# Decoder layer on one core: ten groups of seven products in the second half of each down product, four blocks with five such groups in the first gate/up, earlier folds in the second

## The chip, the core and the metric

The kernel runs on one core of a Trainium2 chip. Its time is the device time of one launch in microseconds (us). Engines: the PE (TensorE) multiplies, DVE (VectorE) adds and subtracts, ACT (ScalarE) casts, copies and evaluates functions, POOL (GpSimd) issues the accumulating DMAs here, and SP (SyncE) issues the loads.

## The reference

One layer for 256 tokens of width 2048, all in float32: a half feed-forward, a mix of retention and windowed attention, a second half feed-forward, and a gated embedding, each followed by a layer norm. The change touches the two feed-forwards:

```python
D_MODEL, SEQ, D_FF = 2048, 256, 5632

def swiglu(x, w_gu, w_down):
    g, u = jnp.split(x @ w_gu, 2, axis=-1)
    return (jax.nn.silu(g) * u) @ w_down

h = layer_norm(alpha * h + 0.5 * swiglu(h, w_ffn1_gu, w_ffn1_down), ...)
...   # retention, attention, mix
h = layer_norm(alpha * h + 0.5 * swiglu(h, w_ffn2_gu, w_ffn2_down), ...)
```

w_gu is 2048 x 11264, w_down 5632 x 2048.

## The kernel before

**Precision.** A float32 product is made of three matmuls on rounded halves: x = hi + lo, and hi·lo, hi·hi and lo·hi are added up in PSUM (`Sum.add`, L510 to L512). The activations' halves stay in memory; each weight chunk (128 x 1024, 512 KB) is loaded once, rounded by ACT (`hf`, L162) and its rest formed by DVE (`lf`, L164). The names of tiles begin with r (raw, as loaded), h and l; `f1_gu_3_0_4` in such a name is the first feed-forward's gate/up, block 3, gate (0) or up (1) columns, pair 4 of the inner dimension.

**Kinds of units.** A stage's inner dimension goes by pairs of 128 rows. For each pair and for a 2 x 2 block of outputs (two halves of the tokens, two groups of 512 columns) there is one unit, and a string of letters says which kind:

- P: two chunks, each split by ACT and DVE; 24 matmuls.
- F: the same 24 matmuls, but the second chunk's rest is made by a fold: ACT multiplies the raw chunk by -1 (`Folding`, L181), POOL issues a DMA that adds the rounded one to it (L182), and ACT makes hi later (`Folded`, L198). It costs DVE one split rather than two.
- S: a group of seven products in place of eight (Strassen's scheme in Winograd's form): 21 matmuls. The weights' sums are made by DVE and ACT: five DVE operations on 512 columns (L279, L280, L285, L289, L294), three on 1024 (L287 `lf`, L296 `luf`, L298 `lvf`), and four casts on ACT (L277, L278, L284 `huf`, L293 `hvf`). The activations' sums ("forms") are made once for each pair. Four extra sums in PSUM (tiles named with s) collect the shared products, and after the last S of a block ACT and DVE combine them (L634, L635, L637 to L639).

**Stages.** A feed-forward has gate/up blocks 0 to 10 of 512 gate and 512 up columns with eight pairs each, then the down product in two halves of 1024 columns with 22 pairs each: the first is written by FIRST_DOWN, the second by SECOND_DOWN, whose last two (f1) or three (f2) pairs are held for the layer norm's part. Gate/up blocks go by `gu_units`: f1's blocks 1 to 10 are "FFSSFSSP"; f2's block 9 is "FSSFSSSP", with a fifth S, for the pair SEVEN_MORE = 4. Each block's gate and up are multiplied and transposed by DMA, and come back as the activations of the down product.

**What sets the order.** All units of the kernel stand in one list, `plan`. `fill` goes ahead of the PE: it issues loads and makes splits in the order of the plan, as long as slots in memory are left (`room`; `slots_for_weights` sets their number by stage, `others` in the down product) and as long as the prepared time is below `ahead`. An S holds seven slots until the PE is done with it, a P's chunk two. `fold_at` puts the begun fold some units ahead of its place: it goes back until the units between take FOLD_AHEAD of time, and in a stretch with S groups on to the next S before that. With FOLD_AHEAD of 0 the multiplication is right ahead of the use. `weave` lets DVE steps of a finished block slip between the steps of a split. All engines run their instructions in the order written, and DVE's, ACT's and SP's lists are set by this plan.

At the start of a second down product DVE first combines the sums of the first (L635 to L639), adds the residual (L1206), adds the other sums (L1241), and takes the statistics (L916).

Of the kernel before, what the change touches and what calls it, by code (L numbers as in the profile page):

```python
# [9 lines left out]
F32R = mybir.dt.float32r  # L10
# [6 lines left out]
P = 128  # L17
S = 256
# [9 lines left out]
KF = FF // P  # L28
# [10 lines left out]
SLOTS = 46  # L39


FOLD_AHEAD = {"f1_gu": 34, "f1_down": 12, "f2_gu": 0, "f2_down": 12}

SEVEN = (0, 1, 2, 3)

# [4 lines left out]

ASIDE_TO = 8

FIVE = {"f1": (), "f2": (9,)}

DELAY = {"f1": 2, "f2": 1}

SEVEN_DOWN = (6, 7, 8, 9)

FIRST_DOWN = "PPPPPFFSFSFSPSFSPSFSPS"
SECOND_DOWN = "PPPSPSPSFSPSFSSPSPPPPP"  # L60
LEAD = 4

BIG = 3.0e38
# [7 lines left out]
def layer(ctx: ExitStack, tc: tile.TileContext, io):  # L71
# [4 lines left out]
    big = ctx.enter_context(tc.tile_pool(name="big", bufs=1))  # L76
# [11 lines left out]
    def slot(shape, dt, name):  # L88
        return slots.tile(shape, dt, tag="slot", name=name)
# [111 lines left out]
    def fold_at(ahead, key):  # L201

        begun = Folding(key)
        at, time = len(plan), 0
        while at > 0 and time < ahead:
            at -= 1
            time += plan[at].time
        if ahead and any(isinstance(u, Seven) for u in plan[at - 12 : at + 1]):
            while not isinstance(plan[at], Seven):
                at -= 1  # L210
        plan.insert(at, begun)
        plan.append(Folded(begun))
# [222 lines left out]
    def slots_for_weights(n, ahead=45, far=90):  # L435
        room.update(slots=n, ahead=ahead, far=far)

    def quiet(on):
        room["quiet"] = on
# [92 lines left out]
    def block_units(units, keys):  # L532

        for kind, p in units:
            if kind == "P":
                plan.extend(Single(keys(n, p)) for n in range(2))
            elif kind == "F":
                plan.append(Single(keys(0, p)))
                fold_at(FOLD_AHEAD[keys(1, p)[0]], keys(1, p))
            else:  # L540
# [39 lines left out]
    def forms_sums(full):  # L580


        n = full.shape[1] // 2
        a11, a21 = (full[:, 0::2, t * P : (t + 1) * P] for t in range(2))
        a12, a22 = (full[:, 1::2, t * P : (t + 1) * P] for t in range(2))
        raw = slot([P, 4 * n, P], F32, "sums")
        f5, f6, f7, f3 = (raw[:, n * j : n * j + n, :] for j in range(4))
        dve.tensor_tensor(f5, a21, a22, ALU.subtract)
        dve.tensor_tensor(f7, a11, a21, ALU.subtract)
        dve.tensor_tensor(f6, f5, a11, ALU.subtract)  # L590
        dve.tensor_tensor(f3, a12, f6, ALU.add)
        return raw

    def forms_split(raw, hi, lo):

        split(hi, lo, raw)
        n = raw.shape[1] // 4
        return lambda e: [(hi[:, n * j + e, :], lo[:, n * j + e, :]) for j in range(4)]

    def seven_forms(full, hi, lo, between=None):  # L600

        raw = forms_sums(full)
        if between is not None:
            between()
        return forms_split(raw, hi, lo)
# [13 lines left out]
    def units_of(order, sevens, ahead=()):  # L619

        sevens, ahead = list(sevens), list(ahead)
        plain = [p for p in range(KD // 2) if p not in sevens + ahead]
        of = {"S": sevens, "D": ahead, "P": plain, "F": plain}
        return [(kind, of[kind].pop(0)) for kind in order]
# [293 lines left out]
    def load_columns(src, col, name):  # L918
        v = slot([P, 2, 512], F32, f"{name}{col}")
        sync.dma_start(v, src[col])  # L920
        return v
# [4 lines left out]
    def load_for_norm(i):  # L926

        vectors.append(ln_vectors(i))
        if i < 2:
            p_raws.append(slot([P, 2, S], F32, "praw"))  # L930
            sync.dma_start(p_raws[0], io["pT"])

    def make_for_norm():
        if p_raws:
            raw, pt = p_raws.pop(), slot([P, 2, 512], F32R, "pt")
            split(pt[:, :, :S], pt[:, :, S:], raw)
            p_parts.append(pt)
# [35 lines left out]
    ht = big.tile([P, KD, 512], F32R, tag="ht", name="xt")  # L973
# [50 lines left out]
    def gu_units(name, j):  # L1024
        if j == 0:
            return [("P", p) for p in range(KD // 2)]
        if name == "f2" and j in AHEAD:
# [3 lines left out]
            return units_of(*((f"P{plain}SDSDSP", SEVEN[:3]) if j % 2 else (f"P{plain}SSDSSP", SEVEN)), AHEAD[j])  # L1031
        if j in FIVE[name]:
            return units_of("FSSFSSSP", SEVEN + (SEVEN_MORE,))
# [6 lines left out]
    def down_units(n_held):  # L1040


        sevens = [2 * g + e for g in SEVEN_DOWN for e in range(2)]
        plain = [p for p in range(KF // 2) if p not in sevens]
        first, second = [], []
        for out, order in ((first, FIRST_DOWN), (second, SECOND_DOWN)):
            n = order.count("S")
            of = {"S": sevens[:n], "P": sorted(plain + sevens[n:], key=lambda p: (p in sevens, p))}
            of["F"] = of["P"]
            out += [(kind, of[kind].pop(0)) for kind in order]  # L1050
            assert not of["S"] and not of["P"]
        return first, second[:-n_held], [p for _, p in second[-n_held:]]
# [4 lines left out]
    def plan_ffn(name):  # L1057
        for j in range(KF // 4):
            block_units(gu_units(name, j), gu_keys(name, j))
        first, second, held = down_units(HELD_PAIRS[name == "f2"])  # L1060
        block_units(first, down_keys(name, 0))
        block_units(second, down_keys(name, 1))
        plan.extend(Single(down_keys(name, 1)(n, p)) for n in range(2) for p in held)

    def ffn(name, i, ht, norm, keep, residual, keepers, away):
# [3 lines left out]
        raws = {}  # L1069
        made = {}  # L1070
# [45 lines left out]
        acts = {}  # L1116

        def convert_high(g):
            hi, lo = (slot([P, 4, S], F32R, f"{name}a{w}{g}") for w in "hl")
            act.copy(hi, raws[g])  # L1120
            acts[g] = hi, lo
            return lambda: dve.tensor_tensor(lo, raws[g], hi, ALU.subtract)
# [4 lines left out]
        for j in range(KF // 4):  # L1127
# [22 lines left out]
            def before(u, j=j, offset=KD // 2 - len(units)):  # L1150
# [7 lines left out]
                if j == 0 and u == 7:  # L1158
                    for g in sorted({p // 2 for p in SEVEN}):
                        hi, lo = (slot([P, 8, P], F32R, f"{name}f{w}{g}") for w in "hl")  # L1160
                        made[g] = seven_forms(keep[g], hi, lo)
                    if FIVE["f1"] and name == "f1":
                        both = slot([P, 2, 4, P], F32R, "f1fm")
# [23 lines left out]
        def others(n, ahead=45):  # L1187

            slots_for_weights(SLOTS - 4 - n - (2 if lazy else 0), ahead, max(90, ahead + 12))

        lhs = lambda k: tuple(a[:, k % 4, :] for a in acts[k // 4])
        y = {}
        space = big.tile([P, 2 * len(SEVEN_DOWN), 8, P], F32R, tag="ht", name=name + "forms")
        made = {}
        first, second, held = down_units(HELD_PAIRS[name == "f2"])
        n_of = {}
        for b, units in enumerate((first, second + [("P", p) for p in held])):
# [17 lines left out]

        def before_unit(u):
            new = [g for g in when if when[g] == u]
            others(2 * KF // 4 - (KF // 4 - len(acts) - len(new)) + (2 if u >= 10 else 0))
            lows = [convert_high(g) for g in new]

            def convert_low():
                for f in lows:
                    f()

            if u % 2 == 0 and 2 <= u < 2 + 2 * len(SEVEN_DOWN):
                at = u // 2 - 1
                made[SEVEN_DOWN[at]] = seven_forms(
                    raws[SEVEN_DOWN[at]], space[:, 2 * at], space[:, 2 * at + 1], convert_low
                )
            else:  # L1230
                convert_low()
            if u in (11, 12):
                y[u - 11] = load_columns(residual, u - 11, name + "y")

        pn = [banks(f"{name}d{n}") for n in range(2)]
        sums = [[Sum(pn[n][t], n_of[0][t, n]) for n in range(2)] for t in range(2)]
        block(f"{name}d0", first, down_keys(name, 0), lhs, forms, sums, fold(0), before_unit)
        weave_all()
        for n in range(2):
# [6 lines left out]
        last_ahead = 136  # L1246
        last = {}
# [1 line left out]
            last[p // 2] = at  # L1249

        def before_unit(u):
            others(2 * sum(at >= u for at in last.values()) + (4 if u < 12 else 9), 45 if u < len(second) - 5 else last_ahead)
            if u in (11, 12):
                y[u - 9] = load_columns(residual, u - 9, name + "y")
            if u == 13:
                load_for_norm(i)
            if u == len(second) - 1:
                make_for_norm()
                quiet(i < 2)

        pt_ = [banks(f"{name}e{t}") for t in range(2)]
        sums = [[Sum(pt_[t][n], n_of[1][t, n]) for n in range(2)] for t in range(2)]
        block(f"{name}d1", second, down_keys(name, 1), lhs, forms, sums, fold(1), before_unit)
        weave_all()
        slots_for_weights(27, last_ahead, last_ahead + 24)
# [803 lines left out]
```

## Time and profile before

| | |
|---|---|
| median of 3 runs | 2228.23 us (2227.85 to 2229.13) |
| profiled execution | 2227.33 us, its span 2225.5 us |
| granted clock of the PE | 0.999 |
| busy: PE, PE weight load | 2214.5 us (100%), 1836.3 us (83%) |
| busy: DVE, ACT, POOL | 1996.5 us (90%), 1452.4 us (65%), 51.0 us (2%) |
| DMA | 575.49 MB, mean 259 GB/s |

Shares are of the span. A busy time counts an engine's instructions without its waits; the PE's matmuls overlap, so their durations add up to more than its time, and what one more of them costs is read from the distance of their starts. A line such as `L635 ... [3.25 <-PE f13s L512]` in a timeline says that the engine sat idle for 3.25 us before this instruction, and that the last thing it waited for was the matmul of L512 on tile f13s. In the list of waits a row has the waiting instruction, what it waited for, the total in us, how often, and the longest.

### The profile page before, as it was taken

Reading aid. Unit: us, or ns where it says so; the run is one execution under the profiler, and the core shown is the slowest. Engines: PE = TensorE matmul, PEld = TensorE weight load, DVE = VectorE, ACT = ScalarE, POOL = GpSimd, SP = SyncE. Lnnn points to the kernel's source line nnn. Section 1 sums busy time; section 2 is a strip of 40 time slices with the busy share of each in tenths; the row PEclk is TensorE's granted clock in tenths of the full one; section 3 lists DMA queues with packets and bytes.
Section 4 is the critical chain, followed back from the end, with each engine's and each line's share of the span. In section 5 each row is a group of like instructions: output and inputs, shape, how many; then the busy total and the mean of one; then the engine's idle time right before and its main releaser. Section 6 shows DMA issues by size and latency. Waiting matters only on the chain.

```text
span 2225.5 us, 29118 instructions
## 1 busy us (share of the span) xinstructions
PE 2214.5 (100%) x10125; PEld 1836.3 (83%) x10125; DVE 1996.5 (90%) x2654; ACT 1452.4 (65%) x1687; POOL 51.0 (2%) x65
## 2 busy tenths in 40 slices
PE   9999999999999999999999999999999999999998
PEld 8888888888888888888788888888888878888887
DVE  6989989989988889789999888779999999899887
ACT  6877777776565545557866567466767678765553
POOL 0000000000000000000000000000000000000000
PEclk9999999999999999999999999999999999999999
DMA  9998998977686889846976578888899899777871
GB/s 312 279 267 243 248 278 229 257 222 249 219 307 235 302 280 330 273 170 226 294 231 234 172 219 319 307 302 265 293 310 312 289 261 276 213 237 238 290 284 68
DMA packets 303771, 575.49 MB, mean 259 GB/s; under 512 B 98812, under 2 KB 103804, under 8 KB 303624
## 3 DMA queue, kind: packets, MB, share of 16 engines
q1 hardware_dynamic: 293576, 541.70, 73.0%
q0 software_dynamic: 8064, 29.36, 7.0%
q10 hardware_dynamic: 1984, 2.58, 0.3%
q8 instruction: 79, 1.29, 0.2%
q14 instruction: 68, 0.56, 0.1%
HBM read 490.20 MB, written 33.55 MB: 235 GB/s over the span
## 4 chain that ended last, share of the span: by engine, by line
PE 95%; DMA 2%; DVE 1%; issue 1%; ACT 0%; ACTq 0%; SPq 0%; DVEq 0%; POOLq 0%
PE f1g L510 3%; PE f1g L512 3%; PE f1g L511 3%; PE rqk L461 3%; PE f1u L510 2%; PE f1u L511 2%; PE f1u L512 2%; PE f2g L512 2%; PE f2g L510 2%; PE f2g L511 2%; PE f2u L512 2%; PE f2u L510 2%; PE f2u L511 2%; PE aqk L461 2%; PE f2e L512 1%; PE f2e L511 1%
## 5 line engine op out<-in xcount | busy, mean ns | idle before, releaser
L164 DVE TENSOR_TENSOR lf_gu<-rf_gu,hf_gu 128x1024 fp32r<-128x1024 f32 x126 | 150.0, 1227 | 29.7 <-ACT hf_gu L162 28.9
L164 DVE TENSOR_TENSOR lw_in_f<-rw_in_f,hw_in_f 128x1024 fp32r<-128x1024 f32 x132 | 158.3, 1221 | 13.6 <-ACT hw_in_f L162 13.5
L162 ACT CAST hf_gu<-rf_gu 128x1024 fp32r<-128x1024 f32 x126 | 127.7, 1050 | 37.6 <-DMA rf_gu<-in_f_gu 31.3
L162 ACT CAST hw_in_f<-rw_in_f 128x1024 fp32r<-128x1024 f32 x132 | 132.9, 1052 | 6.6 <-DMA rw_in_f<-in_w_in_f 3.8
L164 DVE TENSOR_TENSOR lf_down<-rf_down,hf_down 128x1024 fp32r<-128x1024 f32 x96 | 115.9, 1224 | 19.5 <-ACT hf_down L162 16.7
L293 ACT CAST hvf_gu<-vf_gu 128x1024 fp32r<-128x1024 f32 x80 | 84.5, 1056 | 68.7 <-DVE vf_gu L289 65.1
L284 ACT CAST huf_gu<-uf_gu 128x1024 fp32r<-128x1024 f32 x80 | 84.4, 1055 | 65.1 <-DVE uf_gu L280 62.8
L162 ACT CAST hf_down<-rf_down 128x1024 fp32r<-128x1024 f32 x96 | 98.7, 1050 | 25.4 <-DMA rf_down<-in_f_down 12.0
L287 DVE TENSOR_TENSOR lf_gu<-rf_gu,hf_gu 128x1024 fp32r<-128x1024 f32 x80 | 98.1, 1227 | 0.3
L298 DVE TENSOR_TENSOR lvf_gu<-vf_gu,hvf_gu 128x1024 fp32r<-128x1024 f32 x80 | 98.3, 1229 | 0.0
L296 DVE TENSOR_TENSOR luf_gu<-uf_gu,huf_gu 128x1024 fp32r<-128x1024 f32 x80 | 98.3, 1228 | 0.0
L510 PE MATMUL f1g<-hf_gu,xt 128*128 128x512 f32 x232 | 90.5, 390 | 0.4 <-ACT hf_gu L113 0.4
L512 PE MATMUL f1g<-lf_gu,xt 128*128 128x512 f32 x232 | 90.4, 390 | 0.0
L511 PE MATMUL f1g<-hf_gu,xt 128*128 128x512 f32 x232 | 90.3, 389 | 0.0
L277 ACT CAST hf_gu<-rf_gu 128x1024 fp32r<-128x1024 f32 x80 | 83.8, 1048 | 4.6 <-DMA rf_gu<-in_f_gu 4.6
L510 PE MATMUL f2g<-hf_gu,ht 128*128 128x512 f32 x196 | 76.4, 390 | 0.0
L512 PE MATMUL f2g<-lf_gu,ht 128*128 128x512 f32 x196 | 76.3, 389 | 0.0
L511 PE MATMUL f2g<-hf_gu,ht 128*128 128x512 f32 x196 | 76.2, 389 | 0.0
L510 PE MATMUL f1u<-hf_gu,xt 128*128 128x512 f32 x192 | 74.7, 389 | 0.0
L511 PE MATMUL f1u<-hf_gu,xt 128*128 128x512 f32 x192 | 74.7, 389 | 0.0
L512 PE MATMUL f1u<-lf_gu,xt 128*128 128x512 f32 x192 | 74.7, 389 | 0.0
L182 POOL DMA_DIRECT2D lf_gu<-rf_gu x40 | 34.8, 870 | 1632.5 <-PE f2g L511 991.6
(1546 smaller groups left out, 7205.6 us busy)
## 6 DMA issues: line engine op xcount, KB each, us to landing
rf_gu<-in_f_gu SPq DMA_DIRECT2D x362, 512.0 KB
rf_down<-in_f_down SPq DMA_DIRECT2D x176, 512.0 KB
rw_in_f<-in_w_in_f SPq DMA_DIRECT2D x148, 512.0 KB
lf_gu<-rf_gu POOLq DMA_DIRECT2D x40, 512.0 KB, 8.3
rw_rv<-in_w_rv SPq DMA_DIRECT2D x32, 512.0 KB
rw_ret<-in_w_ret SPq DMA_DIRECT2D x32, 512.0 KB
rw_mix<-in_w_mix SPq DMA_DIRECT2D x32, 512.0 KB
rw_pg<-in_w_pg SPq DMA_DIRECT2D x32, 512.0 KB
```

The lines of the kernel that those rows point to most:

```text
L162: act.copy(c.hi, c.raw)
L164: dve.tensor_tensor(c.lo, c.raw, c.hi, ALU.subtract)
L277: act.copy(a.hi, a.raw)
L284: act.copy(uh, u)
L287: dve.tensor_tensor(a.lo, a.raw, a.hi, ALU.subtract)
L293: act.copy(vh, v)
L296: dve.tensor_tensor(ul, u, uh, ALU.subtract)
L298: dve.tensor_tensor(vl, v, vh, ALU.subtract)
L461: pe.matmul(ps[f], hi[:, kk, f * P : (f + 1) * P], rhs(k), start=k == 0, stop=k == n_k - 1,)
L510: pe.matmul(o, al, bh, start=first, stop=False)
L511: pe.matmul(o, ah, bh, start=False, stop=False)
L512: pe.matmul(o, ah, bl, start=False, stop=self.left == 0)
```

## The change

Four tables of letters and numbers change, with what goes along with them:

```diff
-FOLD_AHEAD = {"f1_gu": 34, "f1_down": 12, "f2_gu": 0, "f2_down": 12}
+FOLD_AHEAD = {"f1_gu": 34, "f1_down": 12, "f2_gu": 12, "f2_down": 12}
...
-FIVE = {"f1": (), "f2": (9,)}
+FIVE = {"f1": (3, 5, 7, 9), "f2": (9,)}
...
-SEVEN_DOWN = (6, 7, 8, 9)
-
-FIRST_DOWN = "PPPPPFFSFSFSPSFSPSFSPS"
-SECOND_DOWN = "PPPSPSPSFSPSFSSPSPPPPP"
+SEVEN_DOWN = (6, 7, 8, 9, 5)
+
+FIRST_DOWN = "PPPPFFFSFSFSFSFSPSFSPS"
+SECOND_DOWN = "PPSPSPSFSFSFSSFSSSPPPP"
...
-            of = {"S": sevens[:n], "P": sorted(plain + sevens[n:], key=lambda p: (p in sevens, p))}
+            of = {"S": sevens[:n], "P": sorted(plain + sevens[n:])}
...
-        space = big.tile([P, 2 * len(SEVEN_DOWN), 8, P], F32R, tag="ht", name=name + "forms")
+        space = big.tile([P, 8, 8, P], F32R, tag="ht", name=name + "forms")
...
-            others(2 * KF // 4 - (KF // 4 - len(acts) - len(new)) + (2 if u >= 10 else 0))
+            others(2 * KF // 4 - (KF // 4 - len(acts) - len(new)) + (4 if u >= 10 else 0))
...
-                made[SEVEN_DOWN[at]] = seven_forms(
-                    raws[SEVEN_DOWN[at]], space[:, 2 * at], space[:, 2 * at + 1], convert_low
-                )
+                if at < 4:
+                    hi, lo = space[:, 2 * at], space[:, 2 * at + 1]
+                else:
+                    hi, lo = (slot([P, 8, P], F32R, f"{name}f{w}{u}") for w in "hl")
+                made[SEVEN_DOWN[at]] = seven_forms(raws[SEVEN_DOWN[at]], hi, lo, convert_low)
...
-            others(2 * sum(at >= u for at in last.values()) + (4 if u < 12 else 9), 45 if u < len(second) - 5 else last_ahead)
+            others(2 * sum(at >= u for at in last.values()) + (6 if u < 12 else 11), 45 if u < len(second) - 5 else last_ahead)
```

In f1's blocks 3, 5, 7 and 9 one F becomes an S ("FFSSFSSP" becomes "FSSFSSSP"); the forms of its pair are made in block 0. In the first down product two P become F, with eight S as before; in the second two P become S and two become F (8 S to 10). The fifth group of forms, for activations 5, takes two slots from the pool that the weights share, made at unit 10, so the weights have two fewer from there. f2's folds in gate/up are begun earlier. In all, the PE's rows go from 9942 to 9918, and DVE's from 2592 to 2651.

DVE at the end of f1's block 3, before: the last S (pair 3), then the splits of pair 7 and the first split of block 4, then the combining of block 3's sums.

```order
L296 TENSOR_TENSOR luf1_gu_3_0_3_1441<-uf1_gu_3_0_3_1431,huf1_gu_3_0_3_1440 128x1024
L298 TENSOR_TENSOR lvf1_gu_3_0_3_1447<-vf1_gu_3_0_3_1432,hvf1_gu_3_0_3_1446 128x1024
L164 TENSOR_TENSOR lf1_gu_3_0_7_1467<-rf1_gu_3_0_7_1365,hf1_gu_3_0_7_1466 128x1024
L164 TENSOR_TENSOR lf1_gu_3_1_7_1492<-rf1_gu_3_1_7_1411,hf1_gu_3_1_7_1491 128x1024
L164 TENSOR_TENSOR lf1_gu_4_0_4_1519<-rf1_gu_4_0_4_1452,hf1_gu_4_0_4_1518 128x1024
L635 TENSOR_TENSOR evw_1531<-eve_1530,f13s1_1339 128x512
```

The same place now:

```order
L298 TENSOR_TENSOR lvf1_gu_3_0_3_1412<-vf1_gu_3_0_3_1397,hvf1_gu_3_0_3_1411 128x1024
L279 TENSOR_TENSOR uf1_gu_3_0_4_1437<-rf1_gu_3_1_4_1335 128x512
L280 TENSOR_TENSOR uf1_gu_3_0_4_1437<-rf1_gu_3_0_4_1333,rf1_gu_3_1_4_1335 128x512
L285 TENSOR_TENSOR vf1_gu_3_0_4_1438<-rf1_gu_3_0_4_1333,uf1_gu_3_0_4_1437 128x512
L287 TENSOR_TENSOR lf1_gu_3_0_4_1441<-rf1_gu_3_0_4_1333,hf1_gu_3_0_4_1440 128x1024
L289 TENSOR_TENSOR vf1_gu_3_0_4_1438<-vf1_gu_3_0_4_1438,rf1_gu_3_0_4_1333 128x512
L294 TENSOR_TENSOR bf1_gu_3_0_4_1439<-rf1_gu_3_1_4_1335,bf1_gu_3_0_4_1439 128x512
L296 TENSOR_TENSOR luf1_gu_3_0_4_1447<-uf1_gu_3_0_4_1437,huf1_gu_3_0_4_1446 128x1024
L298 TENSOR_TENSOR lvf1_gu_3_0_4_1453<-vf1_gu_3_0_4_1438,hvf1_gu_3_0_4_1452 128x1024
L164 TENSOR_TENSOR lf1_gu_3_0_7_1484<-rf1_gu_3_0_7_1382,hf1_gu_3_0_7_1483 128x1024
```

Eight DVE instructions for pair 4 stand between pair 3 and pair 7; the one split of pair 4 at the start of the block is gone.

DVE at the start of f1's second down product, before: the end of the statistics, the two splits of the third P (pair 2), and the first S (pair 12).

```order
L916 BN_STATS f1st_4098<-f1y1_4662 128x6 x2
L164 TENSOR_TENSOR lf1_down_2_2_5102<-rf1_down_2_2_5015,hf1_down_2_2_5101 128x1024
L164 TENSOR_TENSOR lf1_down_3_2_5120<-rf1_down_3_2_5033,hf1_down_3_2_5119 128x1024
L279 TENSOR_TENSOR uf1_down_2_12_5135<-rf1_down_3_12_5066 128x512
L280 TENSOR_TENSOR uf1_down_2_12_5135<-rf1_down_2_12_5064,rf1_down_3_12_5066 128x512
```

The same place now:

```order
L916 BN_STATS f1st_4147<-f1y1_4717 128x6 x2
L279 TENSOR_TENSOR uf1_down_2_12_5152<-rf1_down_3_12_5117 128x512
L280 TENSOR_TENSOR uf1_down_2_12_5152<-rf1_down_2_12_5115,rf1_down_3_12_5117 128x512
L285 TENSOR_TENSOR vf1_down_2_12_5153<-rf1_down_2_12_5115,uf1_down_2_12_5152 128x512
L287 TENSOR_TENSOR lf1_down_2_12_5156<-rf1_down_2_12_5115,hf1_down_2_12_5155 128x1024
```

The first S comes right behind the statistics, two splits sooner on DVE, and on the PE one P sooner.

ACT in f2 between block 8 and block 9, before: the fold of pair 5 of block 9 (L181, then L198) stands right ahead of the combining of block 8's sums (L634).

```order
L162 CAST hf2_gu_8_1_7_16301<-rf2_gu_8_1_7_16249 128x1024
L162 CAST hf2_gu_9_0_5_16330<-rf2_gu_9_0_5_16251 128x1024
L181 ACTIVATE lf2_gu_9_1_5_16334<-rf2_gu_9_1_5_16278 128x1024
L198 CAST hf2_gu_9_1_5_16337<-rf2_gu_9_1_5_16278 128x1024
L634 COPY eve_16343<-f28s0_16155 128x512
```

Now:

```order
L181 ACTIVATE lf2_gu_9_1_5_16307<-rf2_gu_9_1_5_16278 128x1024
L277 CAST hf2_gu_8_0_3_16313<-rf2_gu_8_0_3_16280 128x1024
L278 CAST bf2_gu_8_0_3_16312<-rf2_gu_8_1_3_16282 128x512
L284 CAST huf2_gu_8_0_3_16319<-uf2_gu_8_0_3_16310 128x1024
L293 CAST hvf2_gu_8_0_3_16325<-vf2_gu_8_0_3_16311 128x1024
L162 CAST hf2_gu_8_0_7_16356<-rf2_gu_8_0_7_16284 128x1024
L162 CAST hf2_gu_8_1_7_16381<-rf2_gu_8_1_7_16331 128x1024
L162 CAST hf2_gu_9_0_5_16410<-rf2_gu_9_0_5_16333 128x1024
L198 CAST hf2_gu_9_1_5_16414<-rf2_gu_9_1_5_16278 128x1024
L634 COPY eve_16422<-f28s0_16232 128x512
```

The multiplication, and with it POOL's DMA, stands ahead of block 8's last S (pair 3), seven casts sooner.

## The prediction

> **What bounds the kernel now.** I read the page first, then the waits of the PE, then the stages that the change touches by windows, and there the timelines of DVE, ACT and PE. The page has the shares and the chain:
>
> ```profile
> span 2225.5 us, 29118 instructions
> PE 2214.5 (100%) x10125; PEld 1836.3 (83%) x10125; DVE 1996.5 (90%) x2654; ACT 1452.4 (65%) x1687; POOL 51.0 (2%) x65
> PE 95%; DMA 2%; DVE 1%; issue 1%; ACT 0%; ACTq 0%; SPq 0%; DVEq 0%; POOLq 0%
> ```
>
> The chain runs through the PE for 95% of the span. The waits of the PE hold seven rows; the largest, and the only one on a split of a weight by DVE, are
>
> ```profile
> PE f2u L512 <- DMA lf_gu<-rf_gu: 1.8, 3, 1.1
> PE mr1a L512 <- DVE lw_ret L164: 0.5, 1, 0.5
> ```
>
> so in the stages of the change the PE waits only for three folds of the second layer's gate/up. Windows (length; then busy time and count of PE, PEld, DVE, ACT, POOL; clock, DMA share, GB/s) of an f1 block of four, the one block of five that exists (f2 9), two S groups on DVE inside it, and the two second down products:
>
> ```profile
> 339.70:380.50 40.80, 40.80 (x182) 33.80 (x181) 36.58 (x46) 30.12 (x32) 2.59 (x3) 1.00 0.93 258
> 1808.00:1850.00 42.00, 40.35 (x175) 32.31 (x174) 41.77 (x52) 30.54 (x34) 1.74 (x2) 1.00 0.89 257
> 1831.92:1844.70 12.78, 12.78 (x58) 10.58 (x57) 12.78 (x17) 7.10 (x9) 0.00 (x0) 1.00 0.97 267
> 571.50:686.00 114.50, 114.50 (x507) 94.85 (x506) 104.97 (x127) 63.68 (x69) 1.75 (x2) 1.00 0.77 267
> 2008.00:2124.00 116.00, 116.00 (x517) 96.10 (x517) 107.64 (x132) 64.58 (x71) 1.91 (x3) 1.00 0.75 261
> ```
>
> PE is full in all but the block of five, DVE is close behind it. A group of seven trades PE time for DVE time, and the question is whether DVE has it to give.
>
> **The change part by part.** *Matmuls removed.* Eight pairs go from 24 matmuls (P or F) to 21 (S): four in f1's gate/up and two in each second down product, 24 matmuls in all. The price of one:
>
> ```profile
> L510 PE MATMUL f1g<-hf_gu,xt 128*128 128x512 f32 x232 | 90.5, 390 | 0.4 <-ACT hf_gu L113 0.4
> 572.16 0.39 PE L510 MATMUL f1e<-hf_down,f1al 128*128 128x512 f32 x1
> 583.04 0.39 PE L510 MATMUL f1e<-hf_down,f1al 128*128 128x512 f32 x1
> ```
>
> The two starts in the second product stand 48 matmuls (two P) apart: 10.88 / 48 = 0.2267 us a matmul, though each lasts 0.39 us. So 24 matmuls are 24 x 0.2267 = 5.44 us. By their durations they would be 24 x 0.39 = 9.4 us. The Trainium skill ("Perfetto Trace Analysis", Identifying the Most-Contended Engine) says that matmul busy time is no measure, because matmuls are pipelined; by that rule 5.44 is the sum to take, and these rows agree with it.
>
> *What DVE pays.* The window of two S groups gives 12.78 / 2 = 6.4 us for one. The operations of one length in it:
>
> ```profile
> L279 DVE TENSOR_TENSOR uf_gu<-rf_gu 128x512 f32<-128x512 f32 x5 | 3.5, 691 | 0.0
> L298 DVE TENSOR_TENSOR lvf_gu<-vf_gu,hvf_gu 128x1024 fp32r<-128x1024 f32 x5 | 6.1, 1228 | 0.0
> ```
>
> They overlap their neighbours by some 0.09 us (1843.85 to 1844.99, 1.14, in the rows below). An F costs one such split, 1.14 us, a P two, 2.27. F to S costs DVE 5.27 us, P to S 4.14, and P to F gives 1.14 back.
>
> *Blocks of five in f1.* What DVE has to spare in a block of four stands just ahead of L635, where it waits for the last S sums of the PE; beside it the same place ahead of f2's block of five, and that block's end:
>
> ```profile
> 164.44 0.69 DVE L635 TENSOR_TENSOR evw<-eve,f13s 128x512 f32<-128x512 f32 x1 [3.25 <-PE f13s L512]
> 164.62 0.39 PE L512 MATMUL f13s<-luf_gu,f1fh 128*128 128x512 f32 x1
> 327.63 0.69 DVE L635 TENSOR_TENSOR evw<-eve,f17s 128x512 f32<-128x512 f32 x1 [2.18 <-PE f17s L512]
> 1803.23 0.40 PE L512 MATMUL f28s<-luf_gu,f2fh 128*128 128x512 f32 x1
> 1805.86 0.69 DVE L635 TENSOR_TENSOR evw<-eve,f28s 128x512 f32<-128x512 f32 x1
> 1843.85 1.24 DVE L298 TENSOR_TENSOR lvf_gu<-vf_gu,hvf_gu 128x1024 fp32r<-128x1024 f32 x1
> 1844.99 1.24 DVE L164 TENSOR_TENSOR lf_gu<-rf_gu,hf_gu 128x1024 fp32r<-128x1024 f32 x1
> 1845.21 0.43 PE L512 MATMUL f29s<-lvf_gu,f2f2h 128*128 128x512 f32 x1
> ```
>
> From L635 to the end of the fifth lv DVE works without a gap: 1843.85 + 1.24 - 1805.86 = 39.2 us. The PE starts the last S sum of the block before at 1803.23 and reads that lv 174 matmuls later, 174 x 0.2267 = 39.45 us if nothing holds it. So a block of five costs the PE what L635 starts late after that matmul, less 0.2: here 2.63, and the PE lost 41.98 - 39.45 = 2.5. In f1, where DVE has been waiting, L635 even starts 0.18 ahead of that matmul (164.44 against 164.62): no loss, but only 0.4 us of margin. The extra 5.27 us leave DVE 5.27 - 3.25 + 3 x 0.2267 = 2.7 late at the end of a block of five, and the block of four behind it has 3.25 to give (2.18 at the end of block 7): that is why only every second block can be one. Two of the four start late in before, for a chunk that comes late to ACT:
>
> ```profile
> 241.79 1.05 ACT L162 CAST hf_gu<-rf_gu 128x1024 fp32r<-128x1024 f32 x1 [2.25 <-DMA rf_gu<-in_f_gu]
> 285.25 1.05 ACT L162 CAST hf_gu<-rf_gu 128x1024 fp32r<-128x1024 f32 x1 [2.86 <-PE f16s L511]
> 287.77 0.69 DVE L635 TENSOR_TENSOR evw<-eve,f16s 128x512 f32<-128x512 f32 x1 [0.21 <-ACT eve L634]
> ```
>
> Three blocks of 40.80 after 164.62 the same matmul of block 6 stands at 287.02, so L635 ahead of block 7 is 0.75 late, some 0.55 of stall if block 6 ends that way again. Blocks 3 and 5 have their L635 in time. I take 0.7 us for the four together: 12 x 0.2267 - 0.7 = **2.0** us gained. Ends: nothing lost (2.7), or 2.5 lost in each as in f2 9 (2.7 - 10 = -7.3). I stay near the first, since L635 waits for the PE in f1 and for ACT in f2 8. The forms for the fifth pair (four 128x128 operations, one of 512, one cast on ACT, in block 0) stand where DVE has no S yet: nothing, at most their 1 to 2 us if that cover is gone.
>
> *f2's folds.* With the begun fold one S group or more ahead, ACT's multiplication and the accumulating DMA start at least 6.4 us sooner; the waits to be covered are three, 1.8 us together, the longest 1.1. The waits themselves go. But DVE ahead of them is nearly unbroken, with two gaps:
>
> ```profile
> 1754.55 0.69 DVE L279 TENSOR_TENSOR uf_gu<-rf_gu 128x512 f32<-128x512 f32 x1 [2.08 <-PE f27s L512]
> 1771.29 0.69 DVE L279 TENSOR_TENSOR uf_gu<-rf_gu 128x512 f32<-128x512 f32 x1 [1.51 <-DMA rf_gu<-in_f_gu]
> lf_gu<-rf_gu POOLq DMA_DIRECT2D x40, 512.0 KB, 8.3
> ```
>
> With L635 2.63 late in block 9 most of the 1.8 comes back as a wait for lv. The fold's load is queued on SP ahead of S (7,3)'s loads instead of behind, and its slots are held one S longer. I take half, **0.9** gained; ends -0.5 (the 2.08 us gap grows by one load) and +2.5 (nothing comes back).
>
> *First down product.* Two P become F, so DVE gets 2.3 us back, and it pays the fifth group's forms (four adds and a split, about 2.5 us from the 512 and 1024 rows). SP has the same loads. The weights have two slots fewer from u = 10 on. I take 0, with -0.5 and +0.3 as ends.
>
> *Second down products.* Two more S in each are 2 x 2 x 3 matmuls, 2.72 us. What stands against it is the start, where DVE first folds and adds up the first product:
>
> ```profile
> 570.97 0.68 DVE L635 TENSOR_TENSOR evw<-eve,f1d0s 128x512 f32<-128x512 f32 x1
> 580.65 2.35 DVE L164 TENSOR_TENSOR lf_down<-rf_down,hf_down 128x1024 fp32r<-128x1024 f32 x2
> 582.91 0.69 DVE L279 TENSOR_TENSOR uf_down<-rf_down 128x512 f32<-128x512 f32 x1
> 587.05 1.23 DVE L296 TENSOR_TENSOR luf_down<-uf_down,huf_down 128x1024 fp32r<-128x1024 f32 x1
> ```
>
> DVE is tied up from 570.97 to 580.65, 9.7 us. In before a P's splits follow, then S, which has three P of the PE as its lead. Now S stands first, with two P: the PE comes to it at 583.04 and reads ul as its 12th matmul, at 583.04 + 11 x 0.2267 = 585.5. DVE starts S at 580.65 and ends ul 587.05 + 1.23 - 582.91 = 5.4 later, at 586.0. Stall: 0.5 in each product; nothing if DVE gets there sooner, 1.3 if the second P's splits come late to it. Later S groups have DVE's whole lead back: P to S twice and P to F twice are 8.3 - 2.3 = 6.0 us more on DVE, 104.97 + 6.0 = 111 in the 114.5 - 1.4 = 113 of f1. So 2.72 - 1.0 = **1.7** gained; ends 0.1 and 2.7.
>
> Sum: 2.0 + 0.9 + 0 + 1.7 = 4.6 us. The profiled execution has 2225.5 of span and 1.8 outside it, 2227.33; the median of the three runs is 2228.23, 0.9 above it. I forecast 2228.23 - 4.6 = **2223.6**.
>
> **The rivals.** *All of it is hidden* (0.15): no stall at the second products, none in f1, f2's waits gone for good: 5.44 + 1.8 = 7.2, 2221. For it: in blocks 3 and 5 DVE waits 3.25 us. Against it: the 0.4 us of margin.
>
> *DVE becomes the bound at the blocks of five* (0.24, the one on the slower side). Its place is the fifth lv of f1 3, 5, 7 and 9. The blocks of four behind them start 2.7 late, and any idle time of DVE there (the late chunk, the slot's wait of 2.86 us) isn't made up, so the next block of five starts late as f2 9 does. Price 2.5 x 4 + 2 x 0.5 = 11.0 against 5.44 and 0.9: 4.7 slower, 2232.9. It turns from gain to loss when a block of five loses (5.44 + 0.9 - 1.0) / 4 = 1.3 us. For it: fifth S groups hold seven slots where an F held four, loads and casts wait for slots (2.86), and DMA is at 0.93 in the block. Against it: rows 164.44 and 327.63. The same page of the Trainium skill calls the engine of highest occupancy the most contended; DVE's 90% over PEld's 83% speaks for this rival, the waits of the PE on DVE (none here) against it. Its Optimization Strategy section adds that a gap repeated in each block can mean that on-chip memory is short for the next tile, which the 2.86 us row bears out in one place.
>
> *Gain and loss cancel* (0.23): blocks of five lose near 0.7 to 1.3 each and the second products 1.3; between 2225 and 2230.
>
> **How the numbers follow.** My forecast's case has 0.38, 2222 to 2225.5. A measurement tells 0.2% from no change, 4.5 us here, so the forecast lies at the bound: of its 0.38 I count 0.25 as faster and 0.13 as the same. Faster: 0.25 + 0.15 = 0.40. Same: 0.13 + 0.23 = 0.36, and slower 0.24, for the rival's price is a little over the bound. The range goes from the sum of all favourable ends (2.7 + 2.5 + 0.3 + 2.7 = 8.2, 2220) to the second rival, 2233.
>
> **What would show it.** PE rows fewer by 24, and blocks of five 40.1 us long in f1 by windows; if they take 41.5 or more, with PE waiting on lvf_gu or luf_gu, the second rival holds. The row f2u L512 <- DMA lf_gu gone from the waits. At the start of the second products a wait of 0.5 on luf_down. Waits of ACT L162 or L277 on PE (slots) much above those quoted would prove my slots too generous.

## The result, and the profile after

The changed kernel takes 2238.39 us (median of 5 runs, 2234.90 to 2240.98), where before took 2228.23 (5 runs, 2226.36 to 2229.13): slower by 0.46%, ratio 1.0046 with the interval 1.0036 to 1.0057. I had forecast 2223.6. Its runs also scatter more, 6 us against 2.8. The profiled execution, 2240.98, is as long as any of the five, 13.65 above that of before, so the places below hold 3 to 4 us more than the medians.

The page of the changed kernel, its first part and its chain:

```profile
span 2239.2 us, 29212 instructions
PE 2219.9 (99%) x10101; PEld 1832.3 (82%) x10101; DVE 2030.0 (91%) x2713; ACT 1469.0 (66%) x1710; POOL 54.3 (2%) x69
PE 67%; DVE 6%; issue 2%; DMA 1%; ACT 1%; ACTq 0%; SPq 0%; DVEq 0%
```

The 24 matmuls are gone (10125 to 10101 records), yet the chain that ended last now runs through DVE for 6% instead of 1%. (The shares add up to 77%: the page follows this chain back only to about 521 us.) The waits of the PE, the rows of interest:

```profile
PE lnps L780 <- DVE f1y L768: 2.6, 2, 2.2
PE lnps L780 <- DVE f2y L768: 2.5, 2, 2.1
...
PE f1d L512 <- DVE lf_down L164: 1.1, 2, 0.7
PE f2d L512 <- DVE lf_down L164: 0.7, 1, 0.7
PE f19s L512 <- DVE luf_gu L296: 0.7, 1, 0.7
...
PE f19s L510 <- DVE eve L1101: 0.6, 1, 0.6
```

The row f2u L512 on lf_gu is gone, as forecast. What came are waits for DVE, in places that I had not costed. Where the time went is read from the first matmul of each stage in both traces (my arithmetic from the two timelines; the mixers between f1 and f2 give back 1.3 and are left out):

| stretch | gained (-) or lost (+), us | forecast |
|---|---|---|
| f1 gate/up, to block 8 | -1.2 | |
| f1 gate/up, blocks 8 to 10 | +2.8 | both: -2.0 |
| f1 first down product | +1.9 | 0 |
| f1 second down product and the norm behind it | +3.9 | -0.9 |
| f2 gate/up | +3.0 | -0.9 |
| f2 first down product | +1.1 | 0 |
| f2 second down product and the norm behind it | +3.8 | -0.9 |

### The profile page after: what moved, and what is told of

Its sections match the earlier page's. It is cut to its first block, busy times and chain, and to the rows that moved or that the text cites. A ratio compares the mean times of both kernels' runs of the same rounds, so it can differ in the third digit from the quotient of the medians.

```text
span 2239.2 us, 29212 instructions
## 1 busy us (share of the span) xinstructions
PE 2219.9 (99%) x10101; PEld 1832.3 (82%) x10101; DVE 2030.0 (91%) x2713; ACT 1469.0 (66%) x1710; POOL 54.3 (2%) x69
## 4 chain that ended last, share of the span: by engine, by line
PE 67%; DVE 6%; issue 2%; DMA 1%; ACT 1%; ACTq 0%; SPq 0%; DVEq 0%
PE rqk L461 3%; PE f2g L512 2%; PE f2g L510 2%; PE f2g L511 2%; PE aqk L461 2%; PE f2u L510 2%; PE f2u L511 2%; PE f2u L512 2%; PE gt L510 1%; PE rqk L469 1%; PE f2d L512 1%; PE f2d L510 1%; PE f2d L511 1%; PE pg L512 1%; PE rg L510 1%
## 5 line engine op out<-in xcount | busy, mean ns | idle before, releaser
L164 DVE TENSOR_TENSOR lw_in_f<-rw_in_f,hw_in_f 128x1024 fp32r<-128x1024 f32 x132 | 158.2, 1219 | 14.0 <-ACT hw_in_f L162 13.9
L164 DVE TENSOR_TENSOR lf_gu<-rf_gu,hf_gu 128x1024 fp32r<-128x1024 f32 x122 | 144.2, 1220 | 25.0 <-ACT hf_gu L162 24.1
L164 DVE TENSOR_TENSOR lf_down<-rf_down,hf_down 128x1024 fp32r<-128x1024 f32 x80 | 96.4, 1221 | 8.9 <-ACT hf_down L162 5.1
L162 ACT CAST hf_down<-rf_down 128x1024 fp32r<-128x1024 f32 x80 | 82.1, 1048 | 12.7 <-DMA rf_down<-in_f_down 8.7
L510 PE MATMUL f1g<-hf_gu,xt 128*128 128x512 f32 x220 | 86.3, 392 | 0.0
L512 PE MATMUL f1g<-lf_gu,xt 128*128 128x512 f32 x220 | 86.0, 391 | 0.0
L511 PE MATMUL f1g<-hf_gu,xt 128*128 128x512 f32 x220 | 85.9, 390 | 0.0
L512 PE MATMUL f2g<-lf_gu,ht 128*128 128x512 f32 x196 | 76.3, 389 | 0.0
L510 PE MATMUL f1u<-hf_gu,xt 128*128 128x512 f32 x176 | 68.5, 389 | 0.0
L511 PE MATMUL f1u<-hf_gu,xt 128*128 128x512 f32 x176 | 68.5, 389 | 0.0
L512 PE MATMUL f1u<-lf_gu,xt 128*128 128x512 f32 x176 | 68.5, 389 | 0.0
```

What stands on the lines that cost most here:

```text
L162: act.copy(c.hi, c.raw)
L164: dve.tensor_tensor(c.lo, c.raw, c.hi, ALU.subtract)
L510: pe.matmul(o, al, bh, start=first, stop=False)
L511: pe.matmul(o, ah, bh, start=False, stop=False)
L512: pe.matmul(o, ah, bl, start=False, stop=self.left == 0)
```

## The experiments

In all of them "before" was run again on the same chip. Each number below is a median, and the difference is to before on that chip.

### The parts alone

Four kernels, each the kernel before with one part of the change: f2's folds; the four blocks of five; the first down products; the second down products with the fifth group of forms.

```diff
p1  +FOLD_AHEAD "f2_gu": 12
p2  +FIVE "f1": (3, 5, 7, 9)
p3  +FIRST_DOWN = "PPPPFFFSFSFSFSFSPSFSPS"
p4  +SEVEN_DOWN = (6, 7, 8, 9, 5), SECOND_DOWN = "PPSPSPSFSFSFSSFSSSPPPP"
```

> The kernel before with only f2's gate/up folds begun earlier (FOLD_AHEAD of f2_gu 12). Theory A (each part costs by itself, as the starts of the stages in the two traces say): f2's gate/up is where 3.0 us went (its end moved from 6.1 to 9.1 us late), so 3 us slower than before, 2231.3, the wait f2u L512 on lf_gu gone, and DVE idle in f2's blocks 3 to 10 near 12 us rather than 8.8. Theory B (the blocks of five of f1 are the whole cause and the later stages inherit a late DVE): f2 lies a mixer behind f1, inherits nothing, and the run is 0.9 us faster as forecast, 2227.3.

> The kernel before with only the four blocks of five in f1 (3, 5, 7, 9). Theory A: 1.6 us slower at the start of f1's first down product, most of it in block 9, and nothing more behind it: 2229.8. Theory B: the lateness of DVE at the end of block 10 (6.3 us against 3.3) goes on into both down products of f1: 2229.8 at that start and 4 to 6 us more by the end of f1, 2234 to 2236.

> The kernel before with only the new FIRST_DOWN (two P become F; no fifth group of forms). Theory A: the PE waits for lf_down (L164) behind the run of F as in the changed kernel, 1.9 us in f1 and 1.1 in f2: 2231.2. Theory B: those waits were inherited from the gate/up that ends with a late DVE; here none, within 0.3 us of 2228.2.

> The kernel before with only the second down products of the changed kernel (ten S, four F, fifth group of forms, two slots fewer). Theory A: 1.4 us fewer matmuls in each, but the layer norm behind it waits 2.3 us for DVE (lnps L780 on L768) and its first matmuls run slowly, so each loses 3.8 net: 7.7 slower, 2235.9. Theory B: DVE enters the second product in time here, no wait at lnps, 1.7 us faster as forecast, 2226.5.

| part | time | before | difference | interval of the ratio |
|---|---|---|---|---|
| folds of f2 | 2228.86 | 2226.99 | +1.9 | 0.9999 to 1.0016 |
| blocks of five | 2228.91 | 2226.99 | +1.9 | 0.9997 to 1.0014 |
| first products | 2227.71 | 2226.99 | +0.7 | 0.9998 to 1.0019 |
| second products | 2231.17 | 2226.99 | +4.2 | 1.0005 to 1.0022 |

Only the last interval lies clear of 1; the others lean to slower. The differences sum to 8.7 of the changed kernel's 10.2. Theory A is right that no single part holds the loss, but two of its sizes are not: the folds took 1.9 where it said 3, and the second products 4.2, between its 7.7 and theory B's gain of 1.7. It is wrong on the first products: their own trace has no wait for lf_down at all, and f1's first product begins and ends there as early as before. Theory B's point holds there: the changed kernel's 1.9 us in f1's first product are handed on, which c3 below tests. In p2's trace, with the old FIRST_DOWN, 0.8 are lost in it.

The second products alone show the wait at the norm:

```profile
PE lnps L780 <- DVE f2y L768: 2.3, 2, 1.8
...
PE lnps L780 <- DVE f1y L768: 1.2, 2, 0.8
PE f1d1s L512 <- DVE lf_down L287: 1.1, 1, 1.1
```

The last row is the stall at the product's start that I had forecast at 0.5; it is 1.1 in this execution, in f1 alone. The changed kernel has no such row; there that matmul starts 0.45 us after the one before it in place of 0.23.

The run of the first products had a time between 2225.05 and 2237.04, and its profile is of the execution that took 2237.04. That is 9.3 above its median, and 7.3 of it are one wait of the PE, and some 1.8 more lie in the nine matmuls behind it, which start 0.43 us apart. The wait is in f2's gate/up, which p3 leaves as it was:

```profile
1883.74 0.79 PE L512 MATMUL f2u<-lf_gu,ht 128*128 128x512 f32 x1 [7.32 <-DMA lf_gu<-rf_gu]
```

A fold of f2's block 10 that isn't begun early came 7.3 us late.

### What is behind the last S

```diff
-SECOND_DOWN = "PPSPSPSFSFSFSSFSSSPPPP"
+SECOND_DOWN = "PPSPSSFSFSFSSFSSSPPPPP"   # p5, the rest as in the changed kernel
+SECOND_DOWN = "PPPSSFSSFSSFSSFSSPPPPP"   # p6, the rest as in p4
```

> The changed kernel with one P moved from the middle of SECOND_DOWN to its end (PPSPSSFSFSFSSFSSSPPPPP): the same ten S, four F and eight P, but five P behind the last S as before the change. Theory C (the second products lose because one P less of PE work covers DVE's combining of the sums and the start of the layer norm): the waits lnps L780 on L768 (2.6 and 2.5 us) and the slow matmuls behind them go, 3 to 4 us in each product, so 2230 to 2232 against 2238.4. Theory D (they lose because DVE has 6 us more to do in each, wherever it stands): the lateness stays and shows as waits for luf_down or lvf_down in the middle or again at lnps, 2236 to 2240.

> The kernel before with only the second down products changed, ten S and four F as in the change, but three P at the start and five at the end as before (PPPSSFSSFSSFSSFSSPPPPP). Theory C: both covers are back, no wait at f1d1s (1.1) and at lnps (1.2 and 2.3), 2.7 us of matmuls saved, 2224 to 2225 where the run of the change's own string had 2231.2 (before 2227.0 in that session). Theory D: waits for the S of the dense middle, at least 2 us in each product, 2229 or more.

p5: 2230.68 (before 2227.22; ratio 1.0015, 1.0007 to 1.0024), 3.5 slower where the changed kernel is 10.2 slower: 6.7 us of the loss gone by moving one P. p6: 2225.04, 2.2 faster than before (ratio 0.9988, 0.998 to 0.9997), with the same ten S, four F and eight P with which p4 was 4.2 slower. The timelines of DVE and PE at the norm behind f1's second product, first of the changed kernel, then of p6:

```profile
690.88 0.48 DVE L768 SCALAR_TENSOR_TENSOR f1y<-f1y,rstd,ln_b 128x256 f32<-128x256 f32 x1
688.97 0.39 PE L512 MATMUL f1e<-lf_down,f1ah 128*128 128x512 f32 x1
691.51 0.41 PE L780 MATMUL lnps<-ident,f1y 128*128 128x128 f32 x2 [2.15 <-DVE f1y L768]
```

```profile
682.96 0.48 DVE L768 SCALAR_TENSOR_TENSOR f1y<-f1y,rstd,ln_b 128x256 f32<-128x256 f32 x1
684.72 0.39 PE L512 MATMUL f1e<-lf_down,f1ah 128*128 128x512 f32 x1
684.94 0.60 PE L780 MATMUL lnps<-ident,f1y 128*128 128x128 f32 x4
```

With four P behind the last S, DVE ends the first normalized piece 2.4 us after the PE's last matmul began; with five, 1.3 before it. Theory C holds, theory D falls: ahead of the tail the 6 us more on DVE cost nothing in f1, where all 1.4 us of the six matmuls came back, and little in f2, where 0.5 came back. p4 and p6 differ at both ends of the string; that the tail alone matters so much is shown by p5, where one P moves.

### Which block of five, which fold

```diff
+FIVE = {"f1": (3, 5, 7), "f2": (9,)}   # p7, the rest as in before
+... fold_at(12 in f2's blocks 9 and 10, else 0)   # p8, the rest as in before
```

> The kernel before with blocks of five in f1 at 3, 5 and 7 only. Theory E (block 9 alone loses, since it follows a block of four that no longer recovers, and hands its lateness to block 10 and the first down product: 1.0 on luf and lvf of f19, 0.7 on f110, 0.65 on lf_down): 1.3 to 2 us faster than before, 2225 to 2226 on the same chip. Theory F (every block of five loses about what it saves, and the forms made in block 0 cost 1 us besides): the same as with four blocks, 1 to 2 us slower than before.

> The kernel before with f2's folds begun earlier in blocks 9 and 10 only. Theory G (the earlier folds cost in blocks 4 to 8, where no fold was ever late, by holding slots and moving loads ahead of those that DVE waits for, and gain in 9 and 10, where the accumulating DMA is late by 1 us as a rule and by 7.3 in one execution): 0.5 to 1 us faster than before, and no run 5 us above its median. Theory H (the cost is in 9 and 10 themselves, whose S groups wait for DVE in place of the fold): 1.5 to 2 us slower, as with all blocks.

p7: 2225.09, 2.1 faster than before (2227.22; ratio 0.9985, 0.9975 to 0.9995), where four blocks were 1.9 slower: by the medians block 9 alone costs some 4 us, theory E. p2's own trace has 2.4 of them, from the start of block 9 to the end of the first product; the rest isn't located. Windows of the changed kernel, each from the last S sum of one block to that of the next, over block 3 (the first of five), 8 (four) and 9 (five):

```profile
124.10:164.30 40.20, 40.20 (x179) 33.29 (x178) 40.20 (x52) 29.79 (x34) 2.61 (x3) 1.00 0.75 214
326.60:367.40 40.80, 40.80 (x181) 33.78 (x180) 37.84 (x48) 30.32 (x34) 1.72 (x2) 1.00 0.97 250
367.40:410.60 43.20, 41.42 (x179) 32.87 (x178) 42.16 (x53) 31.73 (x35) 2.62 (x3) 1.00 0.82 239
```

Block 3 has both engines full and loses nothing. Block 8 should let DVE catch up, but DVE stood idle in it for loads, and again at the head of block 9:

```profile
331.66 1.23 DVE L164 TENSOR_TENSOR lf_gu<-rf_gu,hf_gu 128x1024 fp32r<-128x1024 f32 x1 [1.32 <-ACT hf_gu L162]
335.61 0.69 DVE L279 TENSOR_TENSOR uf_gu<-rf_gu 128x512 f32<-128x512 f32 x1 [1.53 <-DMA rf_gu<-in_f_gu]
371.08 0.69 DVE L279 TENSOR_TENSOR uf_gu<-rf_gu 128x512 f32<-128x512 f32 x1 [1.04 <-DMA rf_gu<-in_f_gu]
381.33 0.47 PE L510 MATMUL f19s<-hf_gu,xt 128*128 128x512 f32 x1 [0.60 <-DVE eve L1101]
408.63 0.50 PE L512 MATMUL f19s<-luf_gu,f1fm 128*128 128x512 f32 x1 [0.68 <-DVE luf_gu L296]
```

So block 9 began with its L635 1.9 us late, and the PE lost 2.4 against before with what came of it, at the first S (the sums' banks wait for L1101) and at the fifth. Measured in the same way, from the PE's start of the last S sum, L635 is 2.24, 2.45 and 2.25 late at the ends of blocks 3, 5 and 7, and 0.44, -0.18 and 1.94 at the ends of blocks 4, 6 and 8: block 8 gave back 0.3 us, where block 4 gave 1.8 and block 6 2.6. In p7 block 8 ends as late, 1.98, but block 9 with four S loses nothing and has its L635 at -0.05.

p8: 2226.58 against 2227.22 (ratio 0.9997, 0.9988 to 1.0006), 0.6 faster and not clear of none. Begun early in all blocks (p1) it was 1.9 slower. The waits of DVE over f2's gate/up, of before and then of p1:

```profile
DVE uf_gu L279 <- DMA rf_gu<-in_f_gu: 4.6, 4, 1.5
DVE lf_gu L164 <- ACT hf_gu L162: 2.4, 3, 1.7
DVE uf_gu L279 <- PE f27s L512: 2.1, 1, 2.1
```

```profile
DVE lf_gu L164 <- ACT hf_gu L162: 6.8, 4, 2.4
DVE uf_gu L279 <- DMA rf_gu<-in_f_gu: 4.1, 2, 2.5
```

9.1 became 10.9 (12.1 with two smaller rows): the chunk that L164 waits for comes later. p8 has 8.7 (9.9 with such rows). That agrees with theory G, but neither p1's loss nor p8's gain is clear of none; that the loads moved by the early folds are what makes that chunk late is argued from the order, not shown by a run. Nor is the price steady: the PE lost 3.0 us over f2's gate/up in the changed kernel's profile, 1.2 in p1's and in p5's, all with the same folds.

The early folds do one thing that the medians don't show. Of the 182 runs here of kernels without them, before among these, 16 are more than 4 us above their kernel's median in that session, as p3's 2237.04 is; of the 71 runs with early folds in blocks 9 and 10 or in all, none is. That a late fold makes such a run long is shown in one of them, by p3's profile.

### Together

Blocks 3, 5 and 7 of five, p6's second products, folds early in f2's blocks 9 and 10; with the old FIRST_DOWN, and with the new. Then the changed kernel without block 9, and the best of these without the early folds.

```diff
c1  = p6 + p7 + p8, FIRST_DOWN as in before
c2  = c1 with FIRST_DOWN = "PPPPFFFSFSFSFSFSPSFSPS"
c3  = the changed kernel with FIVE "f1": (3, 5, 7)
c4  = c2 with FOLD_AHEAD "f2_gu": 0
```

> The three parts that gained, together: blocks of five in f1 at 3, 5 and 7, f2's earlier folds in blocks 9 and 10 only, ten S in the second products between three P and five P (with the fifth group of forms), and FIRST_DOWN as before the change. If the parts add up (2.1, 0.6 and 2.2 faster): 2222.3 where before has 2227.2, faster by over 0.2%. If they share one reserve of DVE time, less than 3 us together: 2224 or more.

> The same with the changed kernel's FIRST_DOWN. Theory I (the waits for lf_down in the first products were handed on by late gate/up blocks): no such wait in f1, within 0.5 us of the kernel with the old FIRST_DOWN. Theory J (the three F in a row and the fifth group's forms make them): the first products of both layers lose 1 to 2 us each, 2 to 4 us slower than with the old FIRST_DOWN.

> The changed kernel with block 9 of f1 a block of four again. Theory E (block 9 alone loses and hands its lateness on): 3.8 us come back as between the two runs without the other parts, and theory I adds the 1.9 us of f1's first product: 2232.5 to 2234.5 where the changed kernel has 2238. If only the 1.6 us of the changed kernel's own f1 gate/up loss come back, block 9 has little to do with what follows: 2236 to 2237.

> Blocks of five in f1 at 3, 5 and 7, the second products with three P at the start and five at the end, the new FIRST_DOWN, and f2's folds as before the change. The kernel with the folds of blocks 9 and 10 begun earlier besides came out 2.6 us faster than before, not the 4.9 that the parts made alone. If the earlier folds are the part that doesn't add up, this one is 4 us or more faster, 2222.9 or less on a chip where before has 2226.9; if blocks of five and second products share the shortfall, it stays at 2224 to 2225, with a wait f2u L512 on lf_gu of 1 to 2 us again.

| kernel | time | lowest to highest | before | interval of the ratio |
|---|---|---|---|---|
| c1 | 2224.46 | 2223.52 to 2225.70 | 2226.91 | 0.9977 to 0.9994 |
| c2 | 2224.32 | 2222.61 to 2227.38 | 2226.91 | 0.9974 to 0.9992 |
| c3 | 2232.66 | 2229.45 to 2234.71 | 2226.91 | 1.0013 to 1.003 |
| c4 | 2227.00 | 2223.10 to 2233.29 | 2226.98 | 0.9984 to 1.0005 |

c3 is 5.8 slower where the changed kernel is 10.2 slower, 4.4 us back for one S fewer (theories E and I together had 5.7): block 9 itself and what it hands on, since f1's first product, which lost 1.9 in the changed kernel, loses nothing here and nothing in c2, which has the same FIRST_DOWN and the same forms. Theory I holds for f1. In f2 the picture is less clear: the first product lost 1.1 to 1.2 in c1, c2, c3, p5 and the changed kernel, which have early folds, 0.5 in p6, 0.2 in p4 and nothing in c4, which have none; all of these have the fifth group of forms. It lost nothing in p1, p2, p3, p7 and p8, without the forms and the slots that they take. In c4 the PE had just waited for a fold, which gave DVE time. So the forms seem to cost it only when DVE enters late; how much of each, no run separates.

c2 is the fastest of these kernels, 2.6 us below before, where the change is 10.2 above; c1 is not to be told from it. But the parts' gains, 2.1, 2.2 and 0.6, came out half, and both my guesses for c4 missed: without the early folds it got slower and scattered over 10 us. Its profile, 2.6 above its median, has late folds again, 3.8 us where I had 1 to 2:

```profile
PE f2u L512 <- DMA lf_gu<-rf_gu: 3.8, 2, 2.8
```

It and that of c1 also hold 2.8 and 2.7 us lost ahead of f1's block 3. The waits of the PE in the first 200 us of c4:

```profile
PE f1g L512 <- DVE lf_gu L164: 0.5, 1, 0.5
PE f11s L512 <- DVE lf_gu L287: 0.4, 1, 0.4
PE f11s L512 <- DVE lvf_gu L298: 0.2, 1, 0.2
```

In c2's and p7's profiles 0.4 and 0.7 are lost there. All these have the fifth pair's forms in block 0; p3, p4 and p6, without them, lost 0.4 or less. But p7's 0.7 went in the first matmuls, at 7 us, as 0.7 did in p1, which has no such forms. What differs between c4 and p7 comes ahead of the forms: in c4 ACT waited for a load and cast the last chunk ahead of them at 42.65 us, in p7 at 40.00, so the split behind them began on DVE at 55.39 in place of 52.72. Why that load came later stays open, and so does whether this alone makes the sum fall short.

## Why the prediction was wrong

- **The price of a matmul** (0.2267 us) was right. Where DVE kept up, a block of five gained 0.68 us: the changed kernel went from 0.38 late to 0.30 early over block 3 and from 0.52 to 1.20 early over block 7. Block 5 gained 0.23.
- **Blocks of five.** The step that failed is "the block of four behind it has 3.25 to give (2.18 at the end of block 7)". The lateness itself was right, 2.2 to 2.5 for my 2.7. But 3.25 and 2.18 are rows at the ends of blocks 3 and 7; block 8, which stands behind block 7, had nothing left at its end in before. There the last S sum began at 368.62, and L635 came 0.86 later:

```profile
369.48 0.69 DVE L635 TENSOR_TENSOR evw<-eve,f18s 128x512 f32<-128x512 f32 x1 [0.21 <-PE f1g L511]
```

  I had the late chunks of blocks 6 and 8, but counted them only as stall of the next block (0.7 for all four) instead of subtracting them from what the block of four can return. In the changed kernel block 8 returned 0.3. Idle DVE time that was free while DVE waited for the PE anyway is lost once DVE is late. It was my second rival's mechanism (2.5 a block, "any idle time of DVE there (the late chunk, the slot's wait of 2.86 us) isn't made up"), in one block of the four: 2.4 in block 9. Then I stopped at the gate/up's end, and 1.9 more came in the first down product, whose own term, 0, was right by itself (p3: 0.7, not clear of none).
- **The forms of the fifth pair**, costed at nothing with 1 to 2 us "if that cover is gone". In the eight profiles that have them, 0.2 to 2.8 us are lost ahead of block 3; in the changed kernel and p7 none of it behind the first matmuls, so there the forms cost nothing.
- **The second down products.** The start was right: summed over the long distances between starts there, f1 of the changed kernel lost 0.6 for the 0.5 forecast (p4 1.9), and the rest of that product ran at full pace. The term that was missing is the end. I wrote that "later S groups have DVE's whole lead back" and closed the sum in the 114.5 us window, by DVE's total. But the new string has one P less behind the last S. The timelines of before at that place:

```profile
684.07 0.49 DVE L768 SCALAR_TENSOR_TENSOR f1y<-f1y,rstd,ln_b 128x256 f32<-128x256 f32 x1
686.41 0.60 PE L780 MATMUL lnps<-ident,f1y 128*128 128x128 f32 x4
```

  DVE ended at 684.56, 1.85 us ahead of the PE's use of it, and one P less is 5.44 us less of PE work in which to get there. It cost 2.6 and 2.5 in waits, and slow matmuls besides; in f1 3.9 in all where I had 0.9 gained. It is the largest piece, and p5 takes it out. The row at 686.41 stands 0.4 us behind the window's end; a view across that end would have shown it.
- **f2's folds.** The waits that I named went, but the gain of 0.9 turned into a loss of 1.9 (p1, not quite clear of none): the end I gave as -0.5 (the fold's load and slots ahead of DVE's own) was the one to weigh, over all the blocks where folds were never late.

The second rival had the sign, and 4.7 of the 10.2. That it comes so near is in part luck: it priced four losing blocks, of which one lost, and what it lacked was the norm.

## What to carry to other kernels

Where an engine has slack, ask at which instruction it stands and who comes next: the same S groups made the kernel 2.2 us faster in the middle of the second products and 4.2 slower close to their start and end. Once slack is spent, small waits of that engine that were harmless before can become time; subtract them from what it is to give back. When a string of stages changes, follow the sum past the end of the last one to the next point where the slow engine must deliver.

## What the runs showed of the hardware

A short wait of the PE was dearer than itself. After waits of 2.15 and 0.41 us the clock went down. Windows of 6 us about the norm's start in f1, in the changed kernel, in c3 (waits of 1.32 and 0.42), and in p4 (0.75 and 0.42):

```profile
691.00:697.00 6.00, 5.07 (x17) 3.90 (x18) 5.86 (x11) 0.74 (x2) 0.00 (x0) 0.72 0.01 3
```

```profile
686.00:692.00 6.00, 5.04 (x17) 3.84 (x18) 5.86 (x11) 0.75 (x2) 0.00 (x0) 0.72 0.01 3
```

```profile
687.00:693.00 6.00, 4.96 (x25) 4.03 (x26) 5.86 (x11) 1.33 (x3) 0.00 (x0) 1.00 0.01 3
```

The granted clock is 0.72 in the first two and 1.00 in the third. In the changed kernel matmuls then start 0.43 us apart in place of 0.23, for about 3.4 us from 693.32 on, 1.8 us behind the first wait:

```profile
693.74 0.63 PE L511 MATMUL pp<-hw_pp,pt 128*128 128x512 f32 x1
694.17 0.63 PE L512 MATMUL pp<-lw_pp,pt 128*128 128x512 f32 x1
694.59 0.63 PE L510 MATMUL pp<-hw_pp,pt 128*128 128x512 f32 x1
```

That is some 8 matmuls at 0.2 us more, 1.6 us. The Trainium skill ("TensorE: Matmul & The Clock Gate", Part 1) puts the fall to half rate behind at least one idle window of about 3.4 us; here 1.3 us of waiting, with a second short wait behind it, was enough, and for this kernel these rows decide. The half-rate start distance that the page gives, 426.7 ns for 512 columns, agrees with these rows.
